# Retention products of two heads on row blocks, state space outputs in the next inputs' burst, the last heads split on chip, all gates ahead of bc

## The chip, the cores and the metric

The kernel runs on one core of one Trainium2 chip. The metric is the device time of an execution in microseconds (us).

## What is computed

One inference step of a hybrid decoder trunk of two layers, D = 1024, for 560 tokens: a prompt of 512 with 16 meta tokens ahead of it, and eight sampled sequences of four tokens. Each layer is a token mixer of three branches (S5, a complex diagonal state space model of 48 groups; RG-LRU; RetNet retention of eight heads, dk 64, dv 128), each projected and merged by sigmoid gates, and then a gated MLP with a causal convolution. All is fp32. Of the reference, what the change touches:

```python
# S5: one group has 16 inputs and 64 states
y = (jnp.einsum('blgp,gip->blgi', hr, c_re.astype(F32))
     - jnp.einsum('blgp,gip->blgi', hi, c_im.astype(F32)))
y = y.reshape(Bsz, L, S5_WIDTH) + d_skip.astype(F32) * uf
z = jax.nn.gelu(y)
# retention, one chunk
o = jnp.einsum('bhnm,bhme->bhne', scores, v)
o = o + jnp.einsum('bhnd,bhde->bhne', q, s) * jnp.exp(log_gamma[:, None] * (n + 1.0))[..., None]
s_new = jnp.exp(log_gamma * C)[:, None, None] * s + jnp.einsum('bhmd,bhme->bhde', k_dec, v)
# merge
m = (gt[:, :, 0] * (y_a @ p['w_branch_a'])
     + gt[:, :, 1] * (y_b @ p['w_branch_b'])
     + gt[:, :, 2] * (y_c @ p['w_branch_c']))
```

## The kernel before

Activations lie as 128 channels x 560 tokens, eight tiles for D. Each is kept as a rounded part and a remainder in the fp32r format (hh and hl, yh and yl, wh and wl for weights), and every large product is the sum of three, high by high, low by high and high by low, in main PSUM banks (tag m, four buffers, pm in the profile). A weight chunk, 128x1024, serves one output tile; a `unit` (L442) is one output tile, its `half` (L424) 280 tokens, 24 matmuls of 128x280. Weights are streamed by SyncE's DMAs in the order that `_order` (L53) writes out; ScalarE casts wh, VectorE subtracts wl.

Beside the large products run Python generators: `s5_gen` (L805), `lru_gen`, one `ret_gen` (L1165) per pair of heads, `normalize` (L1408) and `load_split` (L1668). A planner steps them while the program is built: `pump` takes a step whenever the planner's clocks for VectorE and ScalarE are less than `DEEP` or `st["shallow"]` us ahead of the one for TensorE; a `yield` is a place at which it may turn to something else, and its value says how many slots of the common pool the next step needs; `finish` runs a generator to its end. Each engine's queue is thus written out in a fixed order at build time. All operations are recorded by a helper, so they all have L134.

**S5.** Per layer there are 12 groups n. `ahead` builds the matrices of a group (Bk, CA, br, then W1 and Dt) in a burst of 48 rows, pe_W (L871). Then V·W1 (L976 to L981), 16 rows on 64x64 blocks, gives the inputs; VectorE rotates, scans and writes the states Hr and Hi; `pe_Y` (L910) multiplies Hr and Hi by CA and V by Dt, and `evac_Y` adds the skip and takes the gelu. All these use one pair of PSUM banks, pz (tag z, one buffer); `bank(2)` waits in the planner until it is free. Y of group n-1 is issued in the loop of group n, behind the update of the sampled states, hn.

**Retention.** There are four head pairs hp per layer, five chunks of 112 tokens; chunk 4 holds the last 80 prompt tokens in rows 0 to 79 and the 32 sampled ones in rows 80 to 111. Per pair: scores kf·qf on 64-row blocks, with the heads alternating; the state products; S for the four chunk ends (16 VectorE operations on 64 partitions, two heads block-diagonal in a 128x256 tile); `outs(c)` (per head the chunk's own product, then S·q over the full array, 128x256); for the sampled sequences ss·qm, and km: eight products of 112 rows whose km is zero but for 32 of them. Then statistics, transposes and a multiplication with sg, and each head's result goes to DRAM (ycd). `load_split` brings the eight back as y and splits them into yh and yl for the branch product bc, of which two units run together first. These small products use px (tag x, two banks).

**Order of a layer.** For each hp (L1592): k and q (except where made before), v, two gc units (the gate of a head), then LRU units. Six gates tc (`NTC`, L30), two bc units, two more tc, six bc; then bb with tb, ta, glu and so on. For hp 0 `normalize` rewrites the hidden state in place: between the two halves of the gc units `free[0]` is set and half 0 is rewritten, step by step between other generators' steps; half 1 is finished between the halves of the first LRU unit (L1587). In the second layer the remainders of those tiles are called fl.

A fp32 matmul is two MATMUL rows in the profile.

## Time and profile before

| | us |
|---|---|
| median of three executions | 2315.74 |
| lowest, highest | 2313.77, 2318.67 |
| profiled execution, device time | 2316.45 |
| its span | 2314.7 |
| TensorE busy | 2258.6 (98%) |
| VectorE busy | 1596.6 (69%) |
| ScalarE busy | 906.5 (39%) |
| GpSimd busy | 334.1 (14%) |

The profile is of one execution. TensorE's busy time is modelled and its rows overlap, so a burst's cost is read from the starts of the rows around it. Mean granted clock of TensorE: 0.992 of full. A wait is put down to the operation that ended last before it.

### The profile page before, as it was taken

How to read it: one execution, taken by the hardware profiler on the slowest of the kernel's cores; microseconds unless marked ns; L12 is line 12 of the kernel's file. 1: busy time of each engine (PE TensorE's matmuls, PEld its weight loads, DVE VectorE, ACT ScalarE, POOL GpSimd, SP SyncE). 2: the span in 40 equal slices, each digit the busy share in tenths (PEclk: the TensorE clock that was granted, in tenths of full speed). 3: DMA queues.
4: the chain of work that ended last, by engine and by line, in shares of the span. 5: the costliest groups of instructions: out<-in, count | busy, mean ns of one | idle time of the engine just before them, and what ended most of it. 6: DMA issues, size and time to landing. Idle time of an engine off the chain costs nothing.

```text
span 2314.7 us, 47168 instructions
## 1 busy us (share of the span) xinstructions
PE 2258.6 (98%) x19128; PEld 2217.8 (96%) x19128; DVE 1596.6 (69%) x3817; ACT 906.5 (39%) x1965; POOL 334.1 (14%) x620
## 2 busy tenths in 40 slices
PE   8999999999999999999989999999999999999997
PEld 8999999999999999999989999999999999999996
DVE  7988799885456844546589888898864667364555
ACT  4344446332435433223333445363324354332231
POOL 3231122012010000000243221120111110000011
PEclk9999999999999999999999999999999999999998
DMA  5332333334243232222333332332333432323231
GB/s 177 119 122 82 99 121 103 114 111 121 83 127 126 99 106 86 84 92 83 114 118 100 123 102 92 120 129 87 118 105 95 139 123 96 113 79 95 83 118 46
DMA packets 77146, 245.91 MB, mean 106 GB/s; under 512 B 14272, under 2 KB 17216, under 8 KB 76928
## 3 DMA queue, kind: packets, MB, share of 16 engines
q1 hardware_dynamic: 52704, 175.98, 23.5%
q0 software_dynamic: 24224, 66.92, 9.5%
q8 instruction: 150, 2.46, 0.4%
q14 instruction: 68, 0.56, 0.1%
HBM read 208.23 MB, written 29.76 MB: 103 GB/s over the span
## 4 chain that ended last, share of the span: by engine, by line
PE 71%; DVE 9%; issue 4%; ACT 2%; DMA 2%; POOL 1%; POOLq 0%; DVEq 0%; ACTq 0%
PE pm L134 66%; PE px L134 3%; PE pz L134 2%; DVE wl L134 1%; DVE r L134 1%; ACT wh L134 1%; DMA y<-ycd 1%; DVE part L134 1%; DVE ga L134 1%; DVE sc L134 0%; DVE fo L134 0%; DVE sums L134 0%; POOL out_y L134 0%; DMA wr<-in_wa 0%; DVE cm L134 0%
## 5 line engine op out<-in xcount | busy, mean ns | idle before, releaser
L134 ACT CAST wh<-wr 128x1024 fp32r<-128x1024 f32 (+3 forms) x347 | 346.8, 1004 | 600.8 <-PE pm L134 473.8
L134 DVE TENSOR_TENSOR wl<-wr,wh 128x1024 fp32r<-128x1024 f32 (+3 forms) x347 | 403.6, 1165 | 186.8 <-ACT wh L134 186.5
L134 PE MATMUL pm<-fh,wh 128*128 128x280 f32 (+2 forms) x1632 | 482.1, 295 | 8.3 <-DVE part L134 3.6
L134 PE MATMUL pm<-mh,wh 128*128 128x280 f32 (+2 forms) x1664 | 484.1, 291 | 0.7 <-DVE gp L134 0.7
L134 PE MATMUL pm<-mh,wl 128*128 128x280 f32 (+2 forms) x1664 | 482.6, 290 | 0.0
L134 PE MATMUL pm<-ml,wh 128*128 128x280 f32 (+2 forms) x1664 | 481.9, 290 | 0.0
L134 PE MATMUL pm<-fl,wh 128*128 128x280 f32 (+2 forms) x1632 | 476.6, 292 | 2.7 <-DVE fl L134 2.7
L134 PE MATMUL pm<-fh,wl 128*128 128x280 f32 (+2 forms) x1632 | 475.6, 291 | 0.0
L134 PEld LDWEIGHTS pm<-fh,wh 128*128 128x128 f32 x1632 | 309.5, 190 | 13.4 <-ACT xi L134 3.8
L134 PEld LDWEIGHTS pm<-mh,wh 128*128 128x128 f32 x1664 | 312.8, 188 | 1.6 <-DVE gp L134 1.0
L134 PEld LDWEIGHTS pm<-ml,wh 128*128 128x128 f32 x1664 | 313.3, 188 | 0.3
L134 PEld LDWEIGHTS pm<-mh,wl 128*128 128x128 f32 x1664 | 313.2, 188 | 0.0
L134 PEld LDWEIGHTS pm<-fl,wh 128*128 128x128 f32 x1632 | 309.4, 190 | 3.4 <-DVE fl L134 3.1
L134 PEld LDWEIGHTS pm<-fh,wl 128*128 128x128 f32 x1632 | 309.6, 190 | 0.1
L134 PE MATMUL pm<-hh,wh 128*128 128x280 f32 x928 | 276.8, 298 | 8.5 <-ACT hh L134 6.4
L134 PE MATMUL pm<-hl,wh 128*128 128x280 f32 x928 | 272.5, 294 | 3.3 <-DVE hl L134 3.3
L134 PE MATMUL pm<-hh,wl 128*128 128x280 f32 x928 | 271.6, 293 | 1.0 <-DVE wl L134 1.0
L134 PEld LDWEIGHTS pm<-hh,wh 128*128 128x128 f32 x928 | 175.8, 189 | 12.8 <-ACT hh L134 8.7
L134 PEld LDWEIGHTS pm<-hl,wh 128*128 128x128 f32 x928 | 175.6, 189 | 4.7 <-DVE hl L134 4.5
L134 PEld LDWEIGHTS pm<-hh,wl 128*128 128x128 f32 x928 | 176.2, 190 | 1.3 <-DVE wl L134 1.3
L134 PE MATMUL pm<-yh,wh 128*128 128x280 f32 (+2 forms) x448 | 133.5, 298 | 3.3 <-ACT yh L134 3.3
L134 PE MATMUL pm<-yl,wh 128*128 128x280 f32 (+2 forms) x448 | 131.3, 293 | 0.8 <-DVE yl L134 0.8
(371 smaller groups left out, 4055.4 us busy)
## 6 DMA issues: line engine op xcount, KB each, us to landing
wr<-in_wa SPq DMA_DIRECT2D x249, 512.0 KB, 3.3
wr<-in_w SPq DMA_DIRECT2D x44, 384.0 KB, 3.1
wr<-in_wd SPq DMA_DIRECT2D x32, 448.0 KB, 3.3
wr<-in_wd SPq DMA_DIRECT2D x16, 512.0 KB, 3.6
ycd<-sg POOLq DMA_DIRECT2D x16, 280.0 KB, 3.1
y<-ycd POOLq DMA_DIRECT2D x16, 280.0 KB, 5.6
ss<-in_rets POOLq DMA_DIRECT2D x16, 256.0 KB, 4.2
out_rets<-ss POOLq DMA_DIRECT2D x16, 256.0 KB, 2.6
```

The costliest lines, as they stand in the source:

```text
L134: return f(out, *a, **k)
```

## The change

- km: `vr`, a small tile, gets rows 80 to 111 of v and k by four DMAs per head pair (32 partitions a head); km is one tile of 64x512, and the eight products have 32 rows, with the heads alternating between two banks. The table kds becomes kdr.
- S: each head's state stays on its own 64 partitions, four tiles of 128x128; the S updates are 5 operations on 128 partitions. `across` multiplies S by q per head on 64-row blocks with 128 columns. For chunks 0 to 3 the own products come first, then those of chunks 1 to 3 across chunks; chunk 4 uses a bank per head.
- Y(n-1) stands ahead of V·W(n) in the same pz, in columns 280 to 420, Dt first; `evac_Y` follows the update of hn. Y(11) alone has a burst of its own.
- Heads 6 and 7 are split from sg on chip; the other six are loaded with up to three loads in flight, and that may begin before the last pair is finished.
- `NTC` is 8: all tc gates stand ahead of bc.
- `normalize` rewrites a half in one go: half 0 between the halves of the gc units, half 1 right behind them. Meanwhile `st["deep"]` is `SHALLOW`, which becomes 2.0; the first LRU unit finishes nothing between its halves.

```diff
@@ -27,7 +27,7 @@
-NTC = 6
+NTC = 8
@@ -311,7 +311,7 @@
-    SLACK, DEEP, SHALLOW = cfg.get("slack", 0.6), cfg.get("deep", 6.0), cfg.get("shallow", 1.0)
+    SLACK, DEEP, SHALLOW = cfg.get("slack", 0.6), cfg.get("deep", 6.0), cfg.get("shallow", 2.0)
@@ -352,7 +352,7 @@
-                    and max(clk["V"], clk["A"]) - clk["P"] < (st["shallow"] if s[2] else DEEP)):
+                    and max(clk["V"], clk["A"]) - clk["P"] < (st["shallow"] if s[2] else st["deep"])):
@@ -907,23 +907,23 @@
-        def pe_Y(n):
-            py = z_ps()
+        def pe_Y(n, pz, alone=False):
             ca, d = CA[n % 2], Dt[n % 2]
+            for a in range(2):
+                P.matmul(pz[:, a, 280:420], lhsT=d[:, a * 128:a * 128 + 128], rhs=V2(n, a), start=True, stop=False)
             for j, x in enumerate(X[n]["H"]):
                 for a, g, h in QUAD:
-                    P.matmul(py[GS[g], a, 0:140], lhsT=ca[j][GS[h], a * 96 + 32:a * 96 + 96], rhs=k3(x)[GS[h], a, 0:140],
-                             start=j == 0, stop=False)
-            for a in range(2):
-                P.matmul(py[:, a, 0:140], lhsT=d[:, a * 128:a * 128 + 128], rhs=V2(n, a), start=False, stop=True)
-            X[n]["py"] = py
+                    P.matmul(pz[GS[g], a, 280:420], lhsT=ca[j][GS[h], a * 96 + 32:a * 96 + 96], rhs=k3(x)[GS[h], a, 0:140],
+                             start=False, stop=alone and j == 1)
+            X[n]["py"] = pz[:, :, 280:420]
@@ -975,10 +975,12 @@
+            if n:
+                pe_Y(n - 1, pz)
             for j in range(2):
                 for a, g, h in QUAD:
                     P.matmul(pz[GS[h], a, j * 140:j * 140 + 140], lhsT=W1[GS[g], a, j * 64:j * 64 + 64], rhs=V2(n, a)[GS[g]],
-                             start=True, stop=True)
+                             start=n + j == 0, stop=j == 1)
             yield 0
             Tc, Ts = (t.rearrange("p (a c) -> p a c", a=2)[:, :, 0:132] for t in x["T"])
@@ -991,12 +993,10 @@
+            if n:
+                evac_Y(n - 1)
             zb["n"] -= 2
             yield 0
-            if n:
-                yield from bank(2)
-                pe_Y(n - 1)
-                zb["Y"] = n - 1
             tt(t1[:, :264], t1[:, :264], t2[:, :264], OP.add)
             tt(t3[:, :264], t3[:, :264], t4[:, :264], OP.subtract)
@@ -1011,8 +1011,6 @@
-                evac_Y(n - 1)
-                zb["n"] -= 2
                 put_z(n - 1)
             yield 1
@@ -1026,8 +1024,9 @@
-        yield 0
-        pe_Y(11)
+        yield from bank(2)
+        yield 0
+        pe_Y(11, z_ps(), True)
         yield 0
@@ -1162,7 +1161,8 @@
-    def ret_gen(l, hp, T, ycd, rp, before):
+    def ret_gen(l, hp, T, ycd, rp, before, straight=None):
@@ -1240,63 +1240,73 @@
-        yield 2
+        yield 3
         ss = [slot("ss") for _ in range(2)]
+
+        vr = slot("vr")
         for h in range(2):
             SQ.dma_start(ss[h][:, :512], I["rets"][l, 2 * hp + h])
+        for h in range(2):
+            SQ.dma_start(vr[32 * h:32 * h + 32, 0:128], T["v"][2][80:112, h * 128:h * 128 + 128])
+            SQ.dma_start(vr[32 * h:32 * h + 32, 128:192], k4[80:112, h * 64:h * 64 + 64])
         S = rp["S"]
         fin = rp["fin"]
-        for h in range(2):
-            b = slice(64 * h, 64 * h + 64)
-            e = slice(h * 128, h * 128 + 128)
-            V.tensor_copy(S[0][b, e], p0[b, 0:128])
-            for c in range(1, 4):
-                stt(S[c][b, e], S[c - 1][b, e], gCT[b, hp, 0:1], p0[b, c * 128:c * 128 + 128], OP.mult, OP.add)
-            stt(fin[b, :], S[3][b, e], gCT[b, hp, 1:2], p4[b, :128], OP.mult, OP.add)
+        V.tensor_copy(S[0], p0[:, 0:128])
+        for c in range(1, 4):
+            stt(S[c], S[c - 1], gCT[:, hp, 0:1], p0[:, c * 128:c * 128 + 128], OP.mult, OP.add)
+        stt(fin, S[3], gCT[:, hp, 1:2], p4[:, :128], OP.mult, OP.add)
         yield 0
         SQ.dma_start(O["retp"][l, hp], fin)
         bn = rp["bn"]
         of = []
-        def outs(c, po):
+        def o_of(c, h):
+            return of[h][:C, c * 128:c * 128 + 128] if c < 4 else of[2][:C, h * 128:h * 128 + 128]
+
+        def own(c, po):
+            for h in range(2):
+                P.matmul(po[h], lhsT=(sc[h][:C, c * C:c * C + C] if c < 4 else sc[2][:C, h * C:h * C + C]), rhs=vs(c, h),
+                         start=c % 4 == 0, stop=False)
+
+        def across(c, po):
             M = C if c < 4 else 80
-            o0 = (c % 2) * 256
             for h in range(2):
-                P.matmul(po[:C, o0 + h * 128:o0 + h * 128 + 128],
-                         lhsT=(sc[h][:C, c * C:c * C + C] if c < 4 else sc[2][:C, h * C:h * C + C]), rhs=vs(c, h),
-                         start=h == 0, stop=c == 0 and h == 1)
-            if c:
-                P.matmul(po[:M, o0:o0 + 256], lhsT=qf[:, c * C:c * C + M], rhs=S[c - 1], start=False, stop=c < 4)
-            if c == 4:
-                for h in range(2):
-                    for s in range(4):
-                        P.matmul(po[:C, h * 128:h * 128 + 128], lhsT=qm[h][:, s * C:s * C + C], rhs=ss[h][:, s * 128:s * 128 + 128],
-                                 start=False, stop=s == 3 and h == 1)
-
-        def stats(c0, n, po):
+                b = slice(64 * h, 64 * h + 64)
+                P.matmul(po[h][:M], lhsT=qf[b, c * C:c * C + M], rhs=S[c - 1][b], start=False, stop=c == 3)
+
+        def stats(c, h, ps):
+            i = c * 2 + h
+            V.bn_stats(bn[:C, i * 6:i * 6 + 6], ps)
+
+        po = [side_ps(), side_ps()]
+        at = lambda c: [x[:C, c * 128:c * 128 + 128] for x in po]
+        for c in range(4):
+            own(c, at(c))
+        for c in range(1, 4):
+            across(c, at(c))
+        yield 2
+        for h in range(2):
             of.append(slot("of"))
-            A.copy(of[-1][:C, :n * 256], po[:C, :n * 256])
-            for i in range(2 * n):
-                V.bn_stats(bn[:C, (c0 * 2 + i) * 6:(c0 * 2 + i) * 6 + 6], po[:C, i * 128:i * 128 + 128])
-
-        po, po2 = side_ps(), side_ps()
-        outs(0, po)
-        outs(1, po)
-        outs(2, po2)
-        outs(3, po2)
+            A.copy(of[h][:C, :512], po[h][:C, :512])
+            for c in range(4):
+                stats(c, h, at(c)[h])
+        yield 0
+        po = [side_ps(), side_ps()]
+        own(4, at(0))
+        across(4, at(0))
+        for s in range(4):
+            for h in range(2):
+                P.matmul(po[h][:C, :128], lhsT=qm[h][:, s * C:s * C + C], rhs=ss[h][:, s * 128:s * 128 + 128],
+                         start=False, stop=s == 3)
+        drop(4)
         yield 2
-        stats(0, 2, po)
-        stats(2, 2, po2)
-        yield 0
-        po = side_ps()
-        outs(4, po)
-        drop(4)
-        yield 3
-        stats(4, 1, po)
-        km = [slot("km") for _ in range(2)]
+        of.append(slot("of"))
         for h in range(2):
-            tt(km[h][:C, :512].rearrange("p (s d) -> p s d", d=64), k4[:C, None, h * 64:h * 64 + 64].to_broadcast([C, 8, 64]),
-               kdsT[:C, 2 * hp + h, :, None].to_broadcast([C, 8, 64]))
+            A.copy(o_of(4, h), po[h][:C, :128])
+            stats(4, h, po[h][:C, :128])
+        km = slot("km")
+        tt(km[:64, :512].rearrange("p (s d) -> p s d", d=64), vr[:64, None, 128:192].to_broadcast([64, 8, 64]),
+           kdrT[:64, hp, :, None].to_broadcast([64, 8, 64]))
@@ -1310,9 +1320,10 @@
-        for h in range(2):
-            for s in range(4):
-                P.matmul(pn[h][:, s * 128:s * 128 + 128], lhsT=km[h][:C, s * 128:s * 128 + 128], rhs=vs(4, h), start=True, stop=True)
+        for s in range(4):
+            for h in range(2):
+                b = slice(32 * h, 32 * h + 32)
+                P.matmul(pn[h][:, s * 128:s * 128 + 128], lhsT=km[b, s * 128:s * 128 + 128], rhs=vr[b, 0:128], start=True, stop=True)
         drop(5)
@@ -1340,15 +1351,22 @@
-            yield 0
-            SQ.dma_start(ycd[hd], sg)
-            drop()
+            if straight is None:
+                yield 0
+                SQ.dma_start(ycd[hd], sg)
+                drop()
+            else:
+                yield 2
+                a, b = slot("yh", FR), slot("yl", FR)
+                split(sg, a, b, ALL, 0.5)
+                drop()
+                straight.append((a, b))
         drop(3)
@@ -1423,7 +1441,6 @@
             if k:
-                yield 0
                 last()
@@ -1547,10 +1564,10 @@
-                      S=[sp.tile([128, 256], FT, name=f"S{l}{c}") for c in range(4)],
+                      S=[sp.tile([128, 128], FT, name=f"S{l}{c}") for c in range(4)],
@@ -1584,18 +1601,19 @@
-                    halves_apart(us, lambda: finish(normed[1], "norm"))
+                    halves_apart(us, lambda: None)
...
-            nl = 0
+            nl, ych_late, rets = 0, [], []
...
-                ret = start(ret_gen(l, hp, T, ycd, rp, ret))
+                ret = start(ret_gen(l, hp, T, ycd, rp, ret, ych_late if hp == 3 else None))
+                rets.append(ret)
@@ -1641,9 +1659,14 @@
-                    halves_apart(gcs, lambda: free.__setitem__(0, True))
-                    free[1] = True
-                    finish(normed[0], "norm")
+                    def rewrite(h):
+                        free[h] = True
+                        finish(normed[h], "norm")
+                    st["deep"] = SHALLOW
+                    halves_apart(gcs, lambda: rewrite(0))
+                    flush()
+                    rewrite(1)
+                    st["deep"] = DEEP
@@ -1665,12 +1688,19 @@
-            def load_split(srcs, out, scale=None):
-                for src in srcs:
-                    yield 3
-                    t = slot("y")
-                    SQ.dma_start(t, src)
+            def load_split(srcs, out, scale=None, there=lambda i: True):
+
+                on, i = [], 0
+                while on or i < len(srcs):
+                    while i < len(srcs) and len(on) < 3 and there(i) and used["n"] + 3 <= NG:
+                        on.append((slot("y"), clk["P"] + 4.5))
+                        SQ.dma_start(on[-1][0], srcs[i])
+                        i += 1
+                    if not on or clk["P"] < on[0][1]:
+                        yield 0 if on else 3
+                        continue
                     yield 2
+                    t = on.pop(0)[0]
@@ -1687,9 +1717,10 @@
             flush()
+            yl = start(load_split(ycd[:6], ych, 0.5, lambda i: rets[i // 2] not in side))
             finish(ret, "ret")
-            yl = start(load_split(ycd, ych, 0.5))
             finish(yl, "yl")
+            ych += ych_late
             mt = [None] * 8
...
```

How the change moves instructions is seen at three places. First VectorE's queue in the first layer, where half 0 of the hidden state is rewritten (hl are the remainders, sg and pm the gc units' gates, tBr, tBi, bt state space tables, kd retention). Before:

```order
L134 TENSOR_TENSOR hl_143<-x_71,hh_142 128x280
L134 TENSOR_TENSOR pm_1202<-pm_1202,rn_110 128x280
L134 SCALAR_TENSOR_TENSOR sg_1167<-sg_1167,pm_1202 128x280
L134 TENSOR_TENSOR tBr_1229<-tBr_1229,sc_56_516 128x24x2
L134 TENSOR_TENSOR bt_513<-tBi_1230,sc_57_517 128x48
L134 TENSOR_TENSOR tBr_1229<-tBr_1229,bt_513 128x24x2
L134 TENSOR_TENSOR tBi_1230<-tBi_1230,sc_56_516 128x24x2
L134 TENSOR_TENSOR bt_513<-tBr_1229,sc_57_517 128x48
L134 TENSOR_TENSOR tBi_1230<-tBi_1230,bt_513 128x24x2
L134 TENSOR_TENSOR wl_1242<-wr_1111,wh_1241 128x1024
L134 TENSOR_TENSOR hl_147<-x_72,hh_146 128x280
L134 TENSOR_TENSOR kd_1283<-px_1191,cst 112x512
```

Now:

```order
L134 SCALAR_TENSOR_TENSOR sg_1183<-sg_1183,pm_1150 128x280
L134 TENSOR_TENSOR hl_143<-x_71,hh_142 128x280
L134 TENSOR_TENSOR hl_147<-x_72,hh_146 128x280
L134 TENSOR_TENSOR hl_154<-x_73,hh_153 128x280
L134 TENSOR_TENSOR hl_158<-x_74,hh_157 128x280
L134 TENSOR_TENSOR hl_162<-x_75,hh_161 128x280
L134 TENSOR_TENSOR hl_169<-x_76,hh_168 128x280
L134 TENSOR_TENSOR hl_173<-x_77,hh_172 128x280
L134 TENSOR_TENSOR hl_177<-x_78,hh_176 128x280
L134 TENSOR_TENSOR pm_1203<-pm_1203,rn_110 128x280
L134 SCALAR_TENSOR_TENSOR sg_1163<-sg_1163,pm_1203 128x280
```

The eight subtractions follow one another, and the tables, wl and kd have gone elsewhere.

Second, TensorE's queue in the first layer around bc, in which yh and yl are the operands and V·W and Y are of groups 5 and 4 of S5. Before, V·W stands inside bc:

```order
L134 MATMUL pm_5509<-yh_5466,wh_5351 128x280
L134 MATMUL pm_5509<-yl_5467,wh_5351 128x280
L134 MATMUL pm_5509<-yh_5466,wl_5352 128x280
L134 MATMUL pz_5562<-V_5039,W_518_5430 64x140 x8
L134 MATMUL pm_5506<-yh_5472,wh_5245 128x280
```

and Y further on, in another pz:

```order
L134 MATMUL pm_5509<-yh_5484,wl_5352 128x280
L134 MATMUL pz_5629<-Hr_5339,CA_1627 64x140 x4
L134 MATMUL pz_5629<-Hi_5340,CA_1628 64x140 x4
L134 MATMUL pz_5629<-V_3688,Dt_1630 128x140 x2
L134 MATMUL pm_5506<-yh_5490,wh_5245 128x280
```

Now both stand in one pz, between the last of the eight gates tc and bc:

```order
L134 MATMUL pm_5571<-hh_176,wl_5322 128x280
L134 MATMUL pz_5598<-V_3791,Dt_1758 128x140 x2
L134 MATMUL pz_5598<-Hr_5390,CA_1755 64x140 x4
L134 MATMUL pz_5598<-Hi_5391,CA_1756 64x140 x4
L134 MATMUL pz_5598<-V_5034,W_520_5466 64x140 x8
L134 MATMUL pm_5660<-yh_5624,wh_5435 128x280
```

Dt, Hr, Hi and V·W are one burst, behind the gates' last product and ahead of the first yh.

Third, ScalarE's queue ahead of the first layer's bc (tg is the tanh of a tc gate, yh the cast of a loaded y). Before, eight such casts begin behind the gate:

```order
L134 COPY Dt_1629<-pz_5387 32x2x32
L134 ACTIVATE tg_5425<-pm_5412 128x280
L134 ACTIVATE yh_5454<-y_5452 128x560
L134 ACTIVATE yh_5460<-y_5458 128x560
L134 ACTIVATE yh_5466<-y_5464 128x560
```

Now:

```order
L134 ACTIVATE tg_5503<-pm_5438 128x280
L134 ACTIVATE yh_5530<-sg_4183 128x560
L134 CAST wh_5534<-wr_5363 128x1024
L134 ACTIVATE tg_5503<-pm_5490 128x280
L134 COPY fin_1711<-Hr_5390 128x2
L134 COPY fin_1711<-Hi_5391 128x2
L134 ACTIVATE tg_5584<-pm_5537 128x280
L134 ACTIVATE tg_5584<-pm_5571 128x280
L134 ACTIVATE yh_5624<-y_5618 128x560
L134 ACTIVATE yh_5630<-y_5620 128x560
L134 ACTIVATE yh_5636<-y_5622 128x560
```

A cast from sg stands between the gates, and the casts of the loaded y begin behind the tanh of the eighth gate.

## Rows read from the trace of the kernel before

**Rows 1.** The page: busy time of each engine; granted clock in 40 slices.
```profile
PE 2258.6 (98%) x19128; PEld 2217.8 (96%) x19128; DVE 1596.6 (69%) x3817; ACT 906.5 (39%) x1965; POOL 334.1 (14%) x620
...
PEclk9999999999999999999999999999999999999998
```

**Rows 2.** Waits of TensorE: what for, us in total, times, longest us.
```profile
PE pz L134 <- DVE hn L134: 4.6, 4, 2.1
...
PE pm L134 <- DVE hl L134: 3.3, 3, 2.5
PE pm L134 <- ACT yh L134: 3.3, 2, 2.2
PE pm L134 <- DVE fl L134: 2.7, 2, 2.4
PE pz L134 <- DVE z L134: 2.3, 2, 1.3
...
PE pz L134 <- DVE xc L134: 0.9, 1, 0.9
PE pm L134 <- DVE yl L134: 0.8, 2, 0.4
```

**Rows 3.** Windows: stretch, us, busy us of five engines, granted clock, DMA, GB/s.
```profile
92.00:100.00 8.00, 5.00 (x32) 4.09 (x32) 7.31 (x20) 3.39 (x11) 0.00 (x0) 0.79 0.18 66
397.00:410.00 13.00, 9.44 (x100) 8.75 (x99) 8.98 (x20) 6.71 (x17) 5.91 (x11) 0.88 0.66 211
410.00:425.00 15.00, 12.86 (x107) 11.95 (x106) 14.24 (x40) 4.95 (x16) 0.33 (x3) 0.87 0.20 72
1250.00:1261.00 11.00, 8.33 (x41) 7.42 (x40) 10.42 (x34) 5.73 (x15) 0.00 (x0) 0.69 0.29 97
```

**Rows 4.** Timeline, TensorE, a km burst: start us, us, engine, line, operation, out<-in.
```profile
290.45 0.28 PE L134 MATMUL pm<-wh,hl 128*112 128x256 f32 x1
290.57 1.95 PE L134 MATMUL px<-v,km 112*128 112x128 f32 x16
...
292.48 0.28 PE L134 MATMUL pm<-wl,hh 128*112 128x256 f32 x1
```

**Rows 5.** Timeline of TensorE around sixteen rows of score products.
```profile
248.42 0.29 PE L134 MATMUL pm<-hh,wl 128*128 128x280 f32 x1
248.64 1.04 PE L134 MATMUL px<-qf,kf 64*112 64x112 f32 x16
...
249.84 0.29 PE L134 MATMUL pm<-hl,wh 128*128 128x280 f32 x1
```

**Rows 6.** Timeline of TensorE around four rows of score products.
```profile
255.79 0.29 PE L134 MATMUL pm<-hh,wl 128*128 128x280 f32 x1
256.01 0.45 PE L134 MATMUL px<-qf,kf 64*112 64x112 f32 x4
...
256.63 0.29 PE L134 MATMUL pm<-hl,wh 128*128 128x280 f32 x1
```

**Rows 7.** Timeline of TensorE in the output products of a head pair.
```profile
282.59 0.60 PE L134 MATMUL px<-S,qf 128*80 128x256 f32 x2
283.02 1.91 PE L134 MATMUL px<-ss,qm 128*112 128x128 f32 x16
```

**Rows 8.** Timeline of TensorE around a V·W burst.
```profile
524.84 0.29 PE L134 MATMUL pm<-hh,wl 128*128 128x280 f32 x1
525.06 0.71 PE L134 MATMUL pz<-V,W 64*64 64x140 f32 x16
...
525.93 0.29 PE L134 MATMUL pm<-hl,wh 128*128 128x280 f32 x1
```

**Rows 9.** Timeline of VectorE ahead of that burst.
```profile
522.93 0.43 DVE L134 TENSOR_TENSOR Hi<-r,r 128x264 f32<-128x264 f32 x1
```

**Rows 10.** The page: DMA issues, KB each, median us to landing.
```profile
ycd<-sg POOLq DMA_DIRECT2D x16, 280.0 KB, 3.1
y<-ycd POOLq DMA_DIRECT2D x16, 280.0 KB, 5.6
```

More of the change, by code (lines that the diff above doesn't have):

```diff
@@ L42 @@
 NVEC = _n
-_CST = [("ident", 128), ("cos", NT), ("sin", NT), ("causal", C), ("smask", C), ("rowf", 16), ("kdec", 16), ("kds", 64), ("g1", 16), ("g2", 16),
+_CST = [("ident", 128), ("cos", NT), ("sin", NT), ("causal", C), ("smask", C), ("rowf", 16), ("kdec", 16), ("kdr", 32), ("g1", 16), ("g2", 16),
         ("maskq", 128), ("gC", 8)]
@@ L208, in tile_hybrid_decoder @@
     kdecT = cc("kdec").rearrange("p (a h) -> p a h", a=2)
-    kdsT = cc("kds").rearrange("p (h s) -> p h s", h=8)
+    kdrT = cc("kdr").rearrange("p (g s) -> p g s", g=4)
     g1T = cc("g1").rearrange("p (a h) -> p a h", a=2)
@@ L236, in tile_hybrid_decoder @@
     live, liveX = set(), set()
-    st = {"raw": 0, "hi": 0, "next": 0, "pool": None, "ahead": 1, "land": 0.0, "paced": False, "shallow": cfg.get("sh0", 1.5), "norm": None}
+    st = {"raw": 0, "hi": 0, "next": 0, "pool": None, "ahead": 1, "land": 0.0, "paced": False, "shallow": cfg.get("sh0", 1.5), "norm": None, "deep": cfg.get("deep", 6.0)}
     BOOT = cfg.get("boot", 3)
@@ L908, in s5_gen @@
         f3 = lambda t: t[:, :280].rearrange("p (a c) -> p a c", a=2)
-        def pe_Y(n):
-            py = z_ps()
+        def pe_Y(n, pz, alone=False):
             ca, d = CA[n % 2], Dt[n % 2]
+            for a in range(2):
+                P.matmul(pz[:, a, 280:420], lhsT=d[:, a * 128:a * 128 + 128], rhs=V2(n, a), start=True, stop=False)
             for j, x in enumerate(X[n]["H"]):
                 for a, g, h in QUAD:
-                    P.matmul(py[GS[g], a, 0:140], lhsT=ca[j][GS[h], a * 96 + 32:a * 96 + 96], rhs=k3(x)[GS[h], a, 0:140],
-                             start=j == 0, stop=False)
-            for a in range(2):
-                P.matmul(py[:, a, 0:140], lhsT=d[:, a * 128:a * 128 + 128], rhs=V2(n, a), start=False, stop=True)
-            X[n]["py"] = py
+                    P.matmul(pz[GS[g], a, 280:420], lhsT=ca[j][GS[h], a * 96 + 32:a * 96 + 96], rhs=k3(x)[GS[h], a, 0:140],
+                             start=False, stop=alone and j == 1)
+            X[n]["py"] = pz[:, :, 280:420]
+            zb["Y"] = n
         def evac_Y(n):
@@ L925, in evac_Y @@
                 stt(z[:, a * 140:a * 140 + 140], V2(n, a), vv(l, "s5_d")[:, 2 * n + a:2 * n + a + 1],
-                    py[:, a, 0:140], OP.mult, OP.add)
+                    py[:, a, :], OP.mult, OP.add)
             A.activation(z[:, :280], z[:, :280], AF.Gelu_apprx_tanh)
@@ L1325, in ret_gen @@
             for h in range(2):
-                o = of[c // 2][:C, (c % 2) * 256 + h * 128:(c % 2) * 256 + h * 128 + 128]
+                o = o_of(c, h)
                 i = c * 2 + h
@@ L1342, in ret_gen @@
             for c in range(5):
-                o = of[c // 2][:C, (c % 2) * 256 + h * 128:(c % 2) * 256 + h * 128 + 128]
+                o = o_of(c, h)
                 P.transpose((pa[:, c * C:c * C + C] if c < 4 else pb[:, 0:C]), o, ident[:C, :C])
@@ L1549, in tile_hybrid_decoder @@
                       fin=sp.tile([128, 128], FT, name=f"fin{l}"),
-                      S=[sp.tile([128, 256], FT, name=f"S{l}{c}") for c in range(4)],
+                      S=[sp.tile([128, 128], FT, name=f"S{l}{c}") for c in range(4)],
                       bn=sp.tile([128, 60], FT, name=f"bn{l}"), mv=sp.tile([128, 20], FT, name=f"mv{l}"),
                       rn=sp.tile([128, 10], FT, name=f"rn{l}"), nb=sp.tile([128, 10], FT, name=f"nb{l}"))
-            for t in rp["qm"] + rp["S"]:
+            for t in rp["qm"]:
                 G.memset(t, 0.0)
@@ L2080, in _pack @@
     kd = np.zeros((C, 2, 8))
-    kds = np.zeros((C, 8, 8))
+    kdr = np.zeros((64, 4, 8))
     g1 = np.zeros((C, 2, 8))
@@ L2089, in _pack @@
             for k in range(4):
-                kds[80 + 4 * s + k, h, s] = gam[h] ** (3.0 - k) * 0.125
+                kdr[32 * (h % 2) + 4 * s + k, h // 2, s] = gam[h] ** (3.0 - k) * 0.125
                 g1[80 + 4 * s + k, 1, h] = gam[h] ** (k + 1.0)
     put("kdec", kd.astype(f))
-    put("kds", kds.astype(f))
+    put("kdr", kdr.astype(f))
     put("g1", g1.astype(f))
```

## The prediction

> **What bounds the kernel now.** I read the page first: TensorE is busy 98% of the span at a granted clock of nine tenths or more in every slice but the last, VectorE 69%, ScalarE 39% and GpSimd 14% [rows 1]. So there are only two ways to win time: fewer or cheaper rows on TensorE, or the removal of stretches in which it waits or runs at its lower clock. The list of waits of TensorE says whose they are [rows 2]; I kept those that lie in the mixer stages, which the change rewrites (from the ta gates through the feed-forward net up to the second layer's gc units, TensorE's order is the same before and after). The windows around those waits show what the total of waits does not: the granted clock there averages 0.69 to 0.88 of full, a mixture of 1.2 and 2.4 GHz [rows 3]. Behind an interruption of the steady products the clock is low for a while, so a short wait costs more than its own length. Time lost so is the window's length by one less its granted clock: 8 x 0.21 = 1.7, 13 x 0.12 = 1.6, 15 x 0.13 = 1.95 and 11 x 0.31 = 3.4 us. Last I measured each small burst that interrupts the steady products, from the start of the last product ahead to the start of the second behind, less two steady steps of 0.13 us (0.12 ahead of the km burst, whose products have 256 columns).
>
> The profiled execution took 2316.45 us, 0.7 more than the median 2315.74; the sum is made against the former.
>
> **km products on row blocks.** Each fp32 matmul is two MATMUL rows. A burst of eight 112-row products takes 292.48 - 290.45 - 0.24 = 1.79 us [rows 4]. The new ones have 32 rows and the heads alternate. The trace has no 32-row product; the nearest are the 64-row score products kf·qf, whose heads alternate too. Eight take 1.42 - 0.26 = 1.16 [rows 5], two 0.84 - 0.26 = 0.58 [rows 6]: 0.097 per product of 112 columns, and 0.39 fixed for a burst that changes to blocks and back. With 128 columns a product is 0.111, so the new burst is 8 x 0.111 + 0.39 = 1.28, 0.51 less. The bounds: if two 32-row blocks don't overlap, 16 x 0.111 + 0.39 = 2.17, 0.38 more; without a fixed part 0.89, 0.90 less. I take the row of the same kind, 1.28.
>
> **S·q on row blocks.** A full-array product of 256 columns takes 283.02 - 282.59 = 0.43 us [rows 7]. For chunks 1 to 3, three (1.29) become one run of six of 128 columns: 6 x 0.111 + 0.39 = 1.06, so -0.23. For chunk 4, 0.43 becomes 2 x 0.111 + 0.39 = 0.61, +0.18. A head pair thus gains 0.51 + 0.23 - 0.18 = 0.56; with eight pairs in two layers **-4.5 us**. Here a rule speaks on the fixed part. Rows 5 and 6 give 0.39 per burst. The Trainium skill (TensorEngine Tiling (Array Packing), section Key Properties) says that a change of tiling mode drains TensorE, which the 0.39 bears out, and its section Theoretical Speedup promises up to 2x for a dimension of 64 or less; by that alone a pair would save half of each: 0.89 + 0.65 + 0.21, 14.0 us in all.
>
> The work beside TensorE costs nothing. Per pair the two km multiplications become one of 64 partitions, the state updates run on 128 partitions instead of twice on 64, both on VectorE, which gets lighter; ScalarE's copies are split by head (and four more table loads), and it is idle 61% of the span. Four small DMAs per pair on GpSimd's queue gather vr a whole stage ahead of km: the cover is chunks 0 to 4 of the outputs, and if they were late km alone would wait, as a side product that the planner can put later.
>
> **Y joins the next V·W burst.** The 22 Y bursts of groups 0 to 10 in both layers lose their own entry and exit. A V·W burst takes 1.09 - 0.26 = 0.83 [rows 8]; its eight 64x64 products of 140 columns fill the array's four quarters, at half of 0.097 x 140/112 = 0.121 each they are 0.48, so 0.34 is fixed. The merged burst pays it once: 22 x 0.34 = **-7.5 us**. Below, nothing is saved if the change inside the burst from Dt's full-array products to quarters costs as much as the entry saved; above, 0.39 each gives -8.6. I take 0.34, V·W's own. Moreover Y no longer needs the z bank a second time, so the four waits of pz for the hn update go (4.6 [rows 2]), with the low clock of the window 410 to 425 (1.95 [rows 3]): **-6.5 us**.
>
> What the merger adds: V·W(n) now stands behind Y(n-1) on TensorE, and so behind H(n-1), which VectorE and ScalarE must have written. Behind it queue all the large products. Before, the tightest of 20 of the 22 bursts had H written (start 522.93, 0.43 long) 1.7 us ahead of its V·W at 525.06 [rows 9, 8]; the others had more. In the other two H came later than V·W; in their old places both would wait, and the planner sets them anew.
>
> **Rewrite of the hidden state.** Before, the hl subtractions stand between state space tables, a wl and kd; now eight follow one another while TensorE does the other half of the gc products. Two gc units give 2 x 24 x 0.13 = 6.2 us of cover for eight of about 0.46 (0.43 for 264 columns [rows 9]), 3.7 us. So the waits for hl (3.3) and fl (2.7) go, and the low clock in 92 to 100 (1.7) and 1250 to 1261 (3.4): **-11.1 us**. If ScalarE's cast came late the wait would return at the first xb unit.
>
> **Split ahead of bc.** In the first layer eight loads of y and their casts stood right ahead of bc: yh 2.2 and yl 0.4, and the low clock of 397 to 410 (1.6): 4.2 [rows 2, 3]. A y load takes 5.6 us after a write of 3.1 [rows 10]. The two gates moved ahead are 2 x 48 x 0.13 = 12.5 us of TensorE, longer than both together, and heads 6 and 7 need neither. The first yh cast still follows the last gate's tanh, but the merged burst, 1.8 us, now lies between that gate and bc (the second place of the change's order). **-4.2 us.** In the second layer no burst lies there, so its 3.3 - 2.2 = 1.1 and 0.4 stay. The four DMAs less were hidden.
>
> **Other waits.** Two waits for z and one for xc (2.3 + 0.9 [rows 2]) stand at the bursts that build B; a z bank that is asked for less often frees half of them, **-1.6 us** (0 to 3.2).
>
> **New waits.** The planner places every side step anew, so some waits will arise. The 13 waits for hl, hn, yh, fl and z come to 16.2 us, 1.25 each; I take three of these and one low-clock stretch of 1.6: **+5.35 us** (0 to the whole -23.4 of the four wait terms taken back). The likeliest place is the first layer's bc, where the build of W stands behind six yl subtractions.
>
> Sum: -4.5 - 7.5 - 6.5 - 11.1 - 4.2 - 1.6 + 5.35 = -30.05; 2316.45 - 30.05 = 2286.4, and less 0.7 for the median **2286 us**.
>
> **The rivals.**
> 1. The waits only move. TensorE's work falls by 12.0, but VectorE, ScalarE and the z bank are as late elsewhere. For it: every removed wait has a next one close behind, and the generators share one planner. Against: the hl run visibly loses what stood between. 2316.45 - 12.0 - 0.7 = 2304.
> 2. 32-row blocks don't overlap. km then costs +0.38 instead of -0.51 a pair, 8 x 0.89 = 7.1: 2293. For it: no such row is in the trace; against: 64-row blocks do overlap.
> 3. Slower: the merged burst waits for H. TensorE would stop at each of 22 bursts until VectorE's scan and multiplications and ScalarE's copies of the group before are done, with all large products behind it. It decides the sign from 30/22 = 1.4 us per burst; at 2 us each, 44 us: 2286 + 44 = 2330. Against: rows 9 and 8, 1.7 us in hand at the tightest, and group n+1 can't start before its tables anyway.
> 4. No gain: the waits move and the fixed part of a burst is due to something else, so that neither mergers nor blocks save: 2316.
>
> **How the numbers follow.** My forecast 0.66, rival 1 0.20, rival 2 0.07, rival 3 0.04, rival 4 0.03. The low end: no new wait (-5.35), all of z and xc (-1.6), the second layer's yh and yl (-1.1 - 0.4), the upper price of merging (-1.1) and half of the three fixed parts a pair unpaid (-4.7): 2286 - 14.25, **2271**. The high end is rival 1's **2304**. Outside lie the upper half of rival 1, rivals 3 and 4 and a few hundredths, 2 in 10. A measurement of this kernel tells about 0.2% (4.6 us) from no change. Faster by over that (below 2311): forecast, rivals 1 and 2, less a hundredth, 0.92; within 0.2%: rival 4 and that hundredth, 0.04; slower 0.04.
>
> **What would show it.** Right: a px burst of vr·km of about 1.3 us; S·q products of two heads starting a few ns apart; 22 merged bursts of about 1.8 us where two stood (V·W's 0.83, eight quarter products of Y at 0.06 each, and two of Dt at 0.43 x 140/256 = 0.235); no waits of TensorE for hl, fl and hn in the mixer, and a granted clock near full in the stretches of rows 3; a yh wait in the second layer alone. Wrong: pz waits of over a microsecond at most merged bursts (rival 3), a vr·km burst of 2 us (rival 2), or a sum of waits and low-clock time in the mixers as before with other names (rival 1).

## The result and the profile after

| | before | changed |
|---|---|---|
| median, us (lowest, highest) | 2317.03 (2313.77, 2318.67) | 2289.14 (2287.37, 2293.2) |
| span of the profiled execution | 2314.7 | 2286.5 |
| mean granted clock | 0.992 | 0.995 |

Each column is of four executions; of the kernel before, that is one more than were known ahead of the prediction. The ratio is 0.9881, 95% interval 0.9869 to 0.9893: 27.6 us faster by it (0.0119 x 2317). The forecast was 2286.

The page of the changed kernel (busy time of each engine; below it the granted clock):

```profile
PE 2241.0 (98%) x19192; PEld 2204.7 (96%) x19192; DVE 1574.9 (69%) x3769; ACT 909.4 (40%) x1977; POOL 341.7 (15%) x636
...
PEclk9999999999999999999999999999999999999998
```

The shares are within one point of those of [rows 1]: nothing in them tells that 28 us went. The waits of TensorE in the changed kernel do:

```profile
PE pm L134 <- ACT hh L134: 6.6, 2, 6.2
PE pm L134 <- DVE part L134: 3.6, 1, 3.6
...
PE pz L134 <- DVE CA L134: 2.3, 4, 1.0
...
PE pm L134 <- DVE wl L134: 1.6, 2, 1.0
...
PE pz L134 <- DVE Hi L134: 1.3, 2, 1.1
PE px L134 <- DVE sg L134: 1.2, 2, 0.9
PE pz L134 <- ACT Dt L134: 1.1, 1, 1.1
PE pm L134 <- ACT yh L134: 1.0, 1, 1.0
PE px L134 <- DVE kd L134: 0.7, 1, 0.7
...
PE pm L134 <- DVE yl L134: 0.4, 1, 0.4
```

Of [rows 2], hn, hl, fl, z and xc are no longer there; yh and yl have one wait each, both in the second layer. In their place stand waits at S5 bursts for CA, Hi and Dt. The windows with the numbers of [rows 3], and two more (1230 to 1241, where the second layer's rewrite now lies, and 477.2 to 480.6; columns as there):

```profile
92.00:100.00 8.00, 8.00 (x65) 8.00 (x64) 7.06 (x18) 6.70 (x18) 1.06 (x2) 1.00 0.28 100
397.00:410.00 13.00, 13.00 (x124) 12.55 (x123) 11.14 (x22) 6.16 (x15) 4.02 (x9) 1.00 0.64 236
410.00:425.00 15.00, 14.72 (x155) 14.39 (x154) 13.83 (x39) 6.69 (x20) 2.08 (x4) 1.00 0.22 66
477.20:480.60 3.40, 3.40 (x30) 3.03 (x20) 3.33 (x9) 0.67 (x2) 0.10 (x1) 0.50 0.25 96
1230.00:1241.00 11.00, 10.36 (x87) 9.61 (x86) 9.83 (x24) 6.33 (x17) 0.56 (x1) 1.00 0.12 27
```

All four stretches of [rows 3] have a counterpart at the full 2.4 GHz. The one low-clock stretch left in the mixers is at 477.2, at 1.2 GHz, behind a merged burst in the first layer's bb products. Its timeline on TensorE:

```profile
473.13 0.29 PE L134 MATMUL pm<-yh,wl 128*128 128x280 f32 x1
474.49 0.74 PE L134 MATMUL pz<-V,Dt 128*128 128x140 f32 x4 [1.07 <-ACT Dt L134]
475.16 0.47 PE L134 MATMUL pz<-Hr,CA 64*64 64x140 f32 x8
476.75 0.47 PE L134 MATMUL pz<-Hi,CA 64*64 64x140 f32 x8 [1.12 <-DVE Hi L134]
477.01 1.03 PE L134 MATMUL pz<-V,W 64*64 64x140 f32 x16
477.97 0.60 PE L134 MATMUL pm<-yh,wh 128*128 128x280 f32 x1
```

The burst waits for the z bank (ScalarE's copy of the next group's Dt out of it, 1.07) and then for Hi (1.12); only the second is rival 3's mechanism, at one burst. On VectorE a subtraction of wl, 1.22 us, stands between the writing of Hr and that of Hi there. Another timeline piece of the changed kernel shows a km burst, and a merged one without a wait:

```profile
212.42 0.29 PE L134 MATMUL pm<-hh,wl 128*128 128x280 f32 x1
212.63 1.16 PE L134 MATMUL px<-vr,km 32*128 32x128 f32 x16
...
213.96 0.29 PE L134 MATMUL pm<-hl,wh 128*128 128x280 f32 x1
...
455.15 0.29 PE L134 MATMUL pm<-yh,wl 128*128 128x280 f32 x1
455.28 0.64 PE L134 MATMUL pz<-V,Dt 128*128 128x140 f32 x4
455.85 0.47 PE L134 MATMUL pz<-Hr,CA 64*64 64x140 f32 x8
456.14 0.42 PE L134 MATMUL pz<-Hi,CA 64*64 64x140 f32 x8
456.38 0.66 PE L134 MATMUL pz<-V,W 64*64 64x140 f32 x16
...
457.19 0.30 PE L134 MATMUL pm<-yl,wh 128*128 128x280 f32 x1
```

Measured as in the prediction, km takes 213.96 - 212.42 - 0.26 = 1.28 us, and Y with V·W 457.19 - 455.15 - 0.26 = 1.78. That the blocks overlap is seen in the rows themselves, which the timeline merges: in the first km burst the rows of the two heads start at 143.836 and 143.842, the next two at 144.049 and 144.056, and from there on a pair every 0.11 us; the rows of S·q start in such pairs too (126.523 and 126.530).

### The profile page after: what moved, and what is told of

Its sections match the earlier page's. It is cut to its first block, busy times and chain, and to the rows that moved or that the text cites. A ratio compares the mean times of both kernels' runs of the same rounds, so it can differ in the third digit from the quotient of the medians.

```text
span 2286.5 us, 47370 instructions
## 1 busy us (share of the span) xinstructions
PE 2241.0 (98%) x19192; PEld 2204.7 (96%) x19192; DVE 1574.9 (69%) x3769; ACT 909.4 (40%) x1977; POOL 341.7 (15%) x636
## 4 chain that ended last, share of the span: by engine, by line
PE 83%; DVE 8%; issue 5%; ACT 2%; POOL 1%; DMA 1%; SPq 0%; POOLq 0%; DVEq 0%; ACTq 0%
PE pm L134 77%; PE px L134 4%; PE pz L134 2%; DVE wl L134 1%; DVE part L134 1%; ACT wh L134 1%; DVE r L134 1%; DVE sc L134 0%; DMA wr<-in_wa 0%; DVE fo L134 0%; DVE yl L134 0%; DVE sums L134 0%; POOL out_y L134 0%; DVE fl L134 0%; DVE u L134 0%
## 5 line engine op out<-in xcount | busy, mean ns | idle before, releaser
L134 PEld LDWEIGHTS pm<-hh,wh 128*128 128x128 f32 x928 | 175.9, 190 | 13.2 <-ACT hh L134 9.0
```

Of the source, the lines that this page charges most:

```text
L134: return f(out, *a, **k)
```

## The experiments

Two theories stood after the result. **Parts:** each part takes away its own waits, so its term can be added or removed by itself. **Order:** every edit makes the planner write another order, and what a part is worth depends on the waits that this order happens to have. Four kernels undo one part of the change each, four put one part alone into the kernel before, one puts in two; two move a constant of the planner and no work; one tries to remove the new waits. All were compared with before on the same chip. Us are (ratio - 1) x 2317, and by the two intervals a difference between two of these kernels is uncertain by some 4 us; the waits are those of TensorE in the profiled execution, in us.

| kernel | ratio (95%) | us | hl, fl | yh, yl | hn, z, xc, xp | CA, Hi, Dt | clock |
|---|---|---|---|---|---|---|---|
| before | 1 | 0 | 6.0 | 4.1 | 7.8 | 0 | 0.992 |
| changed | 0.9881 (0.9869 to 0.9893) | -27.6 | 0 | 1.4 | 0 | 4.7 | 0.995 |
| without merging | 0.9909 (0.9894 to 0.9925) | -21.1 | 0 | 3.8 | 2.2 | 2.3 | 0.994 |
| without the rewrite | 0.9911 (0.9898 to 0.9925) | -20.6 | 5.9 | 2.9 | 0.5 | 3.1 | 0.995 |
| without gates and split | 0.9971 (0.9961 to 0.9982) | -6.7 | 0 | 11.5 | 0 | 6.9 | 0.992 |
| without row blocks | 0.9943 (0.9931 to 0.9956) | -13.2 | 0 | 3.8 | 0 | 4.7 | 0.992 |
| gates and split alone | 0.9996 (0.9988 to 1.0005) | -0.9 | 6.1 | 3.3 | 4.2 | 6.9 | 0.992 |
| row blocks alone | 1.0063 (1.0051 to 1.0075) | +14.6 | 6.6 | 6.8 | 11.9 | 0 | 0.989 |
| merging alone | 0.9977 (0.9968 to 0.9987) | -5.3 | 7.1 | 10.1 | 0 | 4.8 | 0.990 |
| the rewrite alone | 1.0027 (1.0016 to 1.0038) | +6.3 | 0 | 5.8 | 13.4 | 0 | 0.991 |
| merging, gates and split | 0.9966 (0.9953 to 0.9978) | -7.9 | 7.2 | 3.7 | 0 | 7.6 | 0.990 |
| before, constant 0.7 | 1.0093 (1.0080 to 1.0106) | +21.5 | 8.9 | 16.4 | 7.2 | 0.5 | 0.987 |
| changed, constant 0.7 | 0.9891 (0.9877 to 0.9905) | -25.3 | 0 | 2.9 | 0 | 4.9 | 0.995 |
| changed, bursts held back | 0.9889 (0.9874 to 0.9903) | -25.7 | 0 | 2.0 | 0 | 3.9 | 0.993 |

Three things add up to these times: TensorE's work (what each part saves of it is measured in the next section), the total of all its waits, and the time at low clock (the span times 1 minus the mean granted clock). The total of waits is 40.8 us before, 28.5 in the changed kernel, 50.5 with the row blocks alone and 56.6 with the constant at 0.7; the low clock takes 18.5, 11.4, 25.6 and 30.4. The three together give the difference of every profiled span from before within 4.2 us, so what isn't work lies in waits and in the clock, whatever tile a wait is named after.

**Without merging.** The hunks of `pe_Y` and of the S5 loop taken back:

```diff
-            if n:
-                pe_Y(n - 1, pz)
...
+            if n:
+                yield from bank(2)
+                pe_Y(n - 1)
+                zb["Y"] = n - 1
```

> The change with one part undone: Y has its own burst again, behind the update of hn, as before. Theory (each part pays its own term): two bursts of 0.825 and 1.31 us stand again where the merged one takes 1.78, 22 x 0.35 = 7.7 us of TensorE, and the waits of pz for hn with their low clock come back, 6.5: about 14 us slower than the change, 2303. Rival (the waits belong to the planner, not to the part): only TensorE's 7.7 comes back and the waits at the S5 bursts come to the same sum as in the change: 2297.

6.5 us slower than the change: the rival. No hn wait came back in this order (z has 1.4 us and xp, of the next B, 0.8), so what returned is about TensorE's own work.

**Without the rewrite.** The normalize hunks and `SHALLOW` taken back:

```diff
+                yield 0
                 last()
...
-                    halves_apart(gcs, lambda: rewrite(0))
-                    flush()
-                    rewrite(1)
+                    halves_apart(gcs, lambda: free.__setitem__(0, True))
+                    free[1] = True
+                    finish(normed[0], "norm")
```

> The change with the rewrite of the hidden state undone: single steps again, half 1 finished between the halves of the first LRU unit, SHALLOW 1.0. TensorE's work is unchanged. Theory: waits for hl and fl of 6.0 us and the low clock behind them, 5.1, come back: about 11 us slower than the change, 2300. Rival (the waits go away with the lighter VectorE queue of the other parts, not with this one): under 3 us slower, 2289 to 2292.

7.0 us slower, between the two. The hl and fl waits came back at once, 5.9, as the theory had it, and 3.4 of low clock with them; but the change's own low-clock stretch went, and so did some of its waits at the S5 bursts (3.6 instead of 4.7).

**Without gates and split.** `NTC` 6, all eight heads through DRAM, `load_split` one at a time:

```diff
-NTC = 8
+NTC = 6
...
-                ret = start(ret_gen(l, hp, T, ycd, rp, ret, ych_late if hp == 3 else None))
+                ret = start(ret_gen(l, hp, T, ycd, rp, ret, None))
...
-            yl = start(load_split(ycd[:6], ych, 0.5, lambda i: rets[i // 2] not in side))
             finish(ret, "ret")
+            yl = start(load_split(ycd, ych, 0.5))
```

> The change with six tc gates ahead of bc, heads 6 and 7 through DRAM again and loads one at a time. TensorE's work is unchanged. Theory: the first layer's yh and yl waits of 2.6 us come back with low clock of 1.6: about 4 us slower than the change, 2293. Rival (bc was ready anyway once the other parts took their work away from that stretch): no difference, 2289 within 3.

20.9 us slower, far beyond both. The yh wait is 6.85 us in the first layer and 4.24 in the second, and the first shows why. VectorE, ScalarE and TensorE of this kernel:

```profile
396.67 0.90 DVE L134 SCALAR_TENSOR_TENSOR sg<-px,vec,sg 128x448 f32<-128x448 f32 x2
...
402.15 2.86 ACT L134 ACTIVATE yh<-y 128x560 fp32r<-128x560 f32 x4 [8.37 <-DMA y<-ycd]
...
402.87 0.60 PE L134 MATMUL pm<-yh,wh 128*128 128x280 f32 x1 [6.85 <-ACT yh L134]
```

The last pair's sg product ends at 397.6; its way through DRAM takes until 402.15, and TensorE stands 6.85 us. In the kernel before, that product ended at 392.8, 12.7 us ahead of bc; in the change it ends at 400.0, 8.8 us ahead of bc and later than before, though all else is earlier. The change's own order makes the last pair late in the first layer, and this part covers that.

**Without row blocks.** The hunks of the S updates, `outs` and km taken back:

```diff
-                P.matmul(pn[h][:, s * 128:s * 128 + 128], lhsT=km[b, s * 128:s * 128 + 128], rhs=vr[b, 0:128], start=True, stop=True)
+                P.matmul(pn[h][:, s * 128:s * 128 + 128], lhsT=km[h][:C, s * 128:s * 128 + 128], rhs=vs(4, h), start=True, stop=True)
...
-                P.matmul(po[h][:M], lhsT=qf[b, c * C:c * C + M], rhs=S[c - 1][b], start=False, stop=c == 3)
+                P.matmul(po[:M, o0:o0 + 256], lhsT=qf[:, c * C:c * C + M], rhs=S[c - 1], start=False, stop=c < 4)
```

> The change with the retention products as before: km of 112 rows, S of both heads in one 128x256 tile, S·q over the full array. Theory: a head pair's bursts go from 1.24 + 2.78 + 2.72 back to 1.79 + 3.05 + 2.63 us, 0.73 more: 8 x 0.73 = 5.8 us slower than the change, 2295, and the waits stay as they are. Rival (VectorE's state updates, twice as many, make side steps late): waits of several us at the S5 and retention bursts beside that, over 2299.

14.4 us slower: more than the bursts. Waits of 3.0 us for zh, at the end of the second mixer where the change has none, a single CA wait of 2.7 and the low clock (7 us more than in the change, by the mean clocks) make up much of the rest. The time is the rival's, but the mechanism I had named for it, late state updates, is not what these waits show.

**One part alone.** For gates and split, with the change's `load_split` and `straight` besides:

```diff
-NTC = 6
+NTC = 8
...
+            yl = start(load_split(ycd[:6], ych, 0.5, lambda i: rets[i // 2] not in side))
             finish(ret, "ret")
```

> The kernel before with one part alone: eight tc gates ahead of bc, heads 6 and 7 split on chip, three loads in flight. Theory (the part is worth the lateness of the last head pair that it finds): before, the last sg product ends 12.7 us (first layer) and 17.7 us (second) ahead of bc and the waits there are 2.6 and 1.5 us with 1.6 of low clock, so it can win 4 to 6 us: 2312 to 2314. Rival (the part is worth the 22 us that its removal from the change cost, whatever stands beside it): 2296.

No difference (the interval holds 1), which neither had. The last pair now ends 24.1 and 33.6 us ahead of bc, but yh and yl fell by 0.8 us alone, and one wait for Dt of 6.4 us arose at a z burst in the new order. For the row blocks (the change's hunks of `ret_gen`, kds and S):

```diff
+        vr = slot("vr")
...
-            for s in range(4):
-                P.matmul(pn[h][:, s * 128:s * 128 + 128], lhsT=km[h][:C, s * 128:s * 128 + 128], rhs=vs(4, h), start=True, stop=True)
+                P.matmul(pn[h][:, s * 128:s * 128 + 128], lhsT=km[b, s * 128:s * 128 + 128], rhs=vr[b, 0:128], start=True, stop=True)
```

> The kernel before with the retention products on row blocks alone. Theory: 8 x 0.73 = 5.8 us of TensorE, 2312, and where the new steps end the last pair later than 12.7 and 17.7 us ahead of bc, that much less of it, as nothing here covers the trip through DRAM. Rival (the 15.7 us of its removal are its own): 2302.

Slower by 14.6 us, which neither had. TensorE's work is less; its waits:

```profile
PE pz L134 <- DVE hn L134: 7.3, 3, 4.7
...
PE pm L134 <- ACT yh L134: 5.6, 2, 3.3
PE pm L134 <- DVE hl L134: 4.5, 3, 2.6
PE pz L134 <- DVE z L134: 4.1, 3, 3.3
...
PE pm L134 <- DVE tg L134: 3.4, 1, 3.4
```

Against [rows 2] hn, z, yh and hl have all grown, and so has tg, from 1.5. For merging (the change's `pe_Y` and S5 loop):

```diff
+            if n:
+                pe_Y(n - 1, pz)
...
-                yield from bank(2)
-                pe_Y(n - 1)
```

> The kernel before with Y in the next V·W burst alone. Theory: 22 x 0.35 = 7.7 us of TensorE, and the four hn waits with their low clock, 6.5: 2304. Rival (as its removal from the change showed, 7.9 us: TensorE alone, the waits come back under other names): 2310.

5.3 us faster (3.0 to 7.4), short of both and nearest to the rival. The hn and z waits went as they should, and a yh wait of 6.8 us came in at the first layer's bc, where the last pair's product ends only 6.2 us ahead. For the rewrite:

```diff
-                    halves_apart(gcs, lambda: free.__setitem__(0, True))
+                    halves_apart(gcs, lambda: rewrite(0))
...
-                    free[1] = True
-                    finish(normed[0], "norm")
+                    flush()
+                    rewrite(1)
```

> The kernel before with the rewrite of the hidden state alone. Theory: the hl and fl waits with their low clock go, 11.1 us: 2307. Rival (7 us, as its removal from the change showed): 2311.

Slower by 6.3 us, which neither had. The hl and fl waits are gone, and TensorE's list is led by others:

```profile
PE pz L134 <- DVE z L134: 7.8, 4, 3.2
...
PE pz L134 <- DVE hn L134: 5.6, 3, 3.8
PE pm L134 <- ACT yh L134: 5.2, 2, 3.7
```

**Two parts.** Merging with gates and split, as above, in the kernel before:

```diff
-NTC = 6
+NTC = 8
...
+                pe_Y(n - 1, pz)
```

> The kernel before with two parts, Y in the next V·W burst and the split ahead of bc with all gates; retention products and rewrite as before. Theory A (the two are covers for each other: merging frees the z bank and the gates cover a late last pair, which cost merging alone a yh wait of 6.8 us): more than the sum of both alone (5.3 + 1.1): TensorE 7.7, yh and hn waits with their low clock 8 to 10: 2300 to 2303. Theory B (each edit moves the planner's order and the waits come out by chance): near the sum of both alone, 2311, or anything within 10 us of it.

7.9 us faster, near the 6.2 of the two alone: theory B. The waits for yh and yl fell from 10.1 to 3.7, as a cover should make them do, but those for CA, zh and Dt grew by 2.7, 1.9 and 0.6. In the time, these two parts show no cover for each other.

**The order alone.** One constant, in the kernel before and in the changed one:

```diff
-    SLACK, DEEP, SHALLOW = cfg.get("slack", 0.6), cfg.get("deep", 6.0), cfg.get("shallow", 1.0)
+    SLACK, DEEP, SHALLOW = cfg.get("slack", 0.7), cfg.get("deep", 6.0), cfg.get("shallow", 1.0)
```

> The kernel before with one planner constant moved: a generator may be stepped again 0.7 us after its last step's planned end, not 0.6. No work changes, only the order. Theory A: within 5 us of before, 2313 to 2323, as the order is sound and only single bursts shift. Theory B: the order's luck is worth 10 us or more, so the time leaves that span in either direction, with new waits at bc (yh) and the z bank (hn, z).

21.5 us slower, with the same instructions in another order. Its waits:

```profile
PE pm L134 <- ACT yh L134: 16.0, 2, 11.6
PE pm L134 <- ACT hh L134: 6.7, 2, 6.1
PE pz L134 <- DVE hn L134: 5.2, 3, 4.6
```

In the first layer the last pair ends 6.4 us ahead of bc here, not 12.7. The wait of 11.6 is in the second, where the lead is 18.3; GpSimd's queue shows what took it:

```profile
1557.01 0.54 POOL L134 DMA_DIRECT2D ycd<-sg  x1 [1.81 <-PE pz L134]
...
1570.16 1.07 POOL L134 DMA_DIRECT2D zd<-z  x2 [12.47 <-ACT tg L134]
1571.23 3.81 POOL L134 DMA_DIRECT2D y<-ycd  x7
```

The loads of y stand behind a store of z. GpSimd waits 12.47 us ahead of it for ScalarE, which had itself waited 7.11 for VectorE's z; so the first of the loads is issued 3.8 us ahead of bc's start at 1575.0. The order of the kernel before was the better one of these two by far, and nothing in it guards bc.

> The changed kernel with the same planner constant at 0.7 in place of 0.6. Theory A (merging and gates are covers, so that the order matters less): within 5 us of the change, 2284 to 2294. Theory B (the change owes part of its gain to this one order): slower by 8 us or more, 2297 and up.

2.3 us slower by the ratios, whose intervals overlap: theory A. Its yh waits are 2.1 in all (in its quickest execution, 2287.3 us; the median is 2292.9):

```profile
PE pm L134 <- ACT yh L134: 2.1, 2, 1.1
```

**Bursts held back.** The changed kernel, in which the planner waits for its own clock (likewise ahead of pe_W, with the end of `build_C`):

```diff
+            zb["t"] = max(zb["t"], clk["V"], clk["A"])
...
+            while clk["P"] < zb["t"] + 2.5:
+                yield 0
             yield from bank(2)
```

> The changed kernel in which the planner issues the bursts of pe_W, and of Y with V·W, only 2.5 us of its own time after the operands' planned end (CA, W, Dt, H). The change waits at such bursts for CA 2.3, Hi 1.3 and Dt 1.1 us, and lost 1.7 to low clock there. Theory A: most of that goes, 2283 to 2286, below both kernels. Theory B (the order shifts as a whole): the waits turn up at other bursts, 2286 to 2300.

25.7 us faster than before, no better than the change: theory B. The CA and Hi waits went, and Dt has 3.9 instead of 1.1. No version beat the change.

## Why the prediction was right

**TensorE's work** (forecast -12.0) came out as worked, a little larger. Over all undisturbed bursts, each less two steady steps of its own neighbours: km from 1.79 to 1.28 (1.27 to 1.29 in all eight), the 1.28 worked out; chunks 0 to 3 from 3.05 to 2.78 (-0.27, forecast -0.23); chunk 4 from 2.62 to 2.75 (+0.13, forecast +0.18); the merged burst from 0.825 + 1.31 to 1.78 (-0.355, forecast -0.34). That is 8 x (0.51 + 0.27 - 0.13) + 22 x 0.355 = 13.0 us; the 0.73 a pair in the expectations of the runs on row blocks is 0.65 by this measure. The term of S·q in chunk 4 was oversized: its two products stand among others, so a fixed part of 0.39 is too much there. Rival 2 is out: 32-row blocks overlap. The Trainium skill's page TensorEngine Tiling (Array Packing), section Theoretical Speedup, allows up to a factor of two for a dimension of 64 or less; by that alone km would take half of 1.79, an estimate of 0.9 us. The 1.28 measured doesn't reach it: the fixed part is there, as in 64-row bursts.

**The waits and the clock** (forecast -18.05, with 5.35 of new waits) gave the rest: 28.2 less 13.0, -15.2. Those removed were removed as said: hl and fl, hn, the first layer's yh and yl, and the low clock behind them; the second layer's yh and yl stayed, at 1.0 and 0.4. Of z and xc all went, where I had taken half. The term that was too small is that of the new waits: CA, Hi, Dt and kd are 5.4 us, and the waits for sg and wl grew by 1.1; with the low clock at 477.2 (3.4 x 0.5 = 1.7) they make 8.2. Their place, too, was not the first layer's bc but, for the largest, its bb.

The rows removed come to 27.4 (with 2.2 of tg, which I had left standing), less 8.2 is 19.2: 4.0 more than the 15.2. Of these, 1.6 lie at the end: from the start of the last large product to the end of the span it is 17.85 us before and 19.46 in the changed kernel. Another 0.7 is the price I put on low clock: a steady step takes 0.233 us there (twelve steps in 2.80 from 407.08 to 409.88 of the kernel before) and 0.129 at full clock, so such a stretch loses 0.45 of its length and not 0.5. The last 1.7 stay unexplained. Nor did low clock follow every interruption, as my argument reads: around the hn wait of 1.48 us at 490.05 of the kernel before, the granted clock from 483 to 492 is 1.00.

That the sum came so close is in part luck. The rows removed were 4.0 us more than the 23.4 I had taken; the new waits were 2.9 more than 5.35, and 4.0 of what the rows say did not come back as time, so most of the misses cancel. And the planner wrote one order of many: only this one and two near it were timed.

**What the argument had wrong** is not in the sum, but in what its lines mean. I priced each wait as belonging to the part that removes it. The experiments bear this out in one column each: the hl and fl waits are 0 in all seven kernels with the rewrite and 5.9 to 8.9 in the seven without; yh and yl are 3.8 or less with the gates and split, 4.1 to 16.4 without; hn is 0 wherever Y is merged (and in one kernel where it isn't, the change without merging). But the time doesn't follow. Alone, the four parts give -0.9, +14.6, -5.3 and +6.3, a sum of +14.7; taken out singly they cost 6.5, 7.0, 20.9 and 14.4, a sum of 48.8; together they give -27.6. Rival 1, that the waits only move, is what happened to the parts when alone, and to two of them worse than that; it did not happen to the four together. Moving one constant shows the size of it: an order of the kernel before is worth 21.5 us, and with the constant at 0.7 in both kernels the change gains 46.8 us, not 27.6. That the change closes the places at which a poor order shows (bc, the rewrite, the second claim on the z bank) fits the constant's 2.3 us in the changed kernel, within the uncertainty; but that is one neighbour of each, so that the changed kernel is steadier in general stays open.

Rival 3 was met at one burst with 1.1 us, and Hi waits come to 1.3 in all, far from 1.4 at each of 22.

## What to carry to other kernels

Where a planner writes the order, price the work that changes (it is the same in every order), and treat each wait as a property of the order: give new waits a term, and check the gain by shifting a constant that changes no work. A single part, tried alone or taken out alone, can come out with the wrong sign or several times its size. One case shows how: the change's order ends the last head pair late, which another of its parts covers; whether such covers are behind the rest of the difference was not shown. Small products that leave half of the array's rows idle are worth pairing where enough of them stand together to pay the fixed part: eight of km cost 0.51 us less, the two of chunk 4 0.13 more. Grouping bursts saves that part once for each.

## What was not expected of the hardware

Two 32-row blocks with alternating heads cost the same as two of 64 rows: eight products of 128 columns took 1.28 us in the burst shown, which is what 0.097 us for 112 columns and 0.39 fixed, measured on 64-row blocks, had given. Dt's full-array products ahead of the quarter products in one burst cost no second fixed part: one fixed part of 0.34, twice 0.48 for the quarter products and 0.47 for Dt (two at 0.43 x 280/512) come to 1.77, and 1.78 was measured.
